# First stage of an encoder layer: lo parts and additions on VectorE alone, blocks of 2, 2, 4, 4, 4 k-tiles, modulation sums 512 columns wide

## The chip, the cores and the metric

The kernel runs on one core of a Trainium2 chip. The metric is the device time of one execution in microseconds (us). Three runs of the kernel before took 2361.72 to 2369.96 us, with a median of 2366.24 us. Engines are named as in the profile: PE is TensorE, DVE VectorE, ACT ScalarE, POOL GpSimd, SP SyncE (which issues the loads from HBM).

## The reference

One layer of an encoder for 512 tokens of width 2048, in float32. A condition vector c gives, through w_ada (2048 x 12288), six modulation vectors (shift, scale and gate for two sub-layers). The part at hand is the beginning:

```
mod = silu(c) @ w_ada + b_ada                       # 2048 -> 12288; sh1, sc1 are the first two parts
h = rms_norm(x, g_norm1) * (1 + sc1) + sh1          # 512 x 2048
proj = h @ w_in                                     # 2048 -> 3904: q, k, v of 8 heads, then the latents
```

Behind it stand differential attention (8 heads), latent attention (8 heads), the output projection, and a SwiGLU feed-forward network of width 5632 with its own norm and modulation.

## The kernel before

Every product of two float32 matrices is made from three products. Each factor is split into a part hi, rounded to the matmul's format (ScalarE casts it), and a rest lo = raw - hi, and the kernel sums hi x hi + lo x hi + hi x lo in PSUM (`mm3`, lines 240 to 243; for the activations the parts are called hh and hl). Weights come through the class `Weights`: `load` issues the DMA into one of three raw buffers, `split` casts hi and has lo subtracted on the engine that the plan names (line 98), `get` keeps one weight tile split ahead and one more loading. There are two buffers each for hi and lo. A weight tile of the first stage is [128, 2 k-tiles x 384 columns]: q, k and v of one head.

The modulation of the first norm is a matrix-vector product, made on VectorE. `ada_sum` (lines 292 to 311) loads w_ada in tiles of 128 x 1024 (512 KB, five buffers called araw) and adds each of the 16 row groups, scaled by an element of c, into an accumulator adaacc (line 308, the first of a sum by line 305). For a block of nk k-tiles the sum is nk x 128 columns wide, and there are two, scale and shift. TensorE then turns the sums into columns (`ada_columns`, line 327), VectorE makes G1 and SH1 from them (lines 328 to 330), and `modulation` transposes x for each k-tile (line 378), applies G1 and SH1 on ScalarE (line 380, xt), casts hh and subtracts hl (line 382).

The 16 k-tiles of the contraction go in blocks (`BLOCKS`), since the modulation of all of them would come too late. In each block the loop runs over five heads (`FIRST`); for each head `head_block` multiplies the block's k-tiles for four token tiles into four PSUM banks and adds the banks to what the head has so far (raw_in, raw_s). The first block is copied by ScalarE (line 486). In later blocks two of four token tiles are added by VectorE straight from PSUM (line 492) and two (`POOL_ADDS`) are copied by ScalarE (line 489) and added by GpSimd (line 490); in the last block all four are VectorE's. The last block is made only for head 0 here, and for heads 1 to 4 as filler within the attention of the heads before them.

Beside the matmuls of block i the loop spreads the sums of block i + 2 (generator `ahead`, over the first 0.9 of the block) and, from 0.2 of the block on, the columns, transposes and splits of block i + 1 (`near`). Before the loop come x, its norm, and the sums of the first two blocks.

Only TensorE's order is as written (`ORDERED`); the other engines' orders, and SyncE's queue of loads, are made by the framework's scheduler from the order of the code and expected times. Each engine then works through its own queue in order. TensorE's banks are in two sets of four that take turns from head to head (`next_tag`).

`W.busy` (line 669) is set to 8 when an attention head begins: the next eight weight tiles that the plan gives to GpSimd get their lo part from VectorE.

Of the kernel before, what the change touches and what calls it, by code (L numbers as in the profile page):

```python
# [10 lines left out]
F32 = mybir.dt.float32  # L11
F32R = mybir.dt.float32r
AF = mybir.ActivationFunctionType
ALU = mybir.AluOpType
# [4 lines left out]
P = 128  # L19
# [3 lines left out]
KC = D // P  # L23
# [13 lines left out]
T2_BUFS = 4  # L37
FIRST = 5
NEAR = 0.2
POOL_ADDS = (1, 3)  # L40
LOADS = "aaaxxxxaxxxxaxxxxaxxxxwaa"
BLOCKS = ((0, 2), (2, 2), (4, 2), (6, 2), (8, 2), (10, 2), (12, 4))
PARTS = (2, 4, 4, 4, 4, 4)
STRAIGHT = 2
X_SLOTS = 24
# [92 lines left out]
def weight_plan(a):  # L138
    w_in = a["w_in"][0]
    qkv = w_in[:, 0:3 * H * P].rearrange("(k p) (s n) -> p k s n", p=P, s=3)  # L140
    plan = []

    def rows(w, r0, nk, c0, n):
        return w[r0:r0 + nk * P, c0:c0 + n].rearrange("(k p) n -> p k n", p=P)

    def add_in(h, j):
        plan.append((("in", h, j), [2, 384], qkv[:, 2 * j:2 * j + 2, :, h * P:(h + 1) * P], "pool"))

    for k0, nk in BLOCKS:
        for h in range(FIRST):  # L150
            for j in range(k0 // 2, (k0 + nk) // 2):
                add_in(h, j)
    for h in range(FIRST, H):
        for j in range(KC // 2):
            add_in(h, j)
    c0 = 3 * H * P
    for i in range(2):
        for j in range(KC // 4):
            plan.append((("cq", i, j), [4, 256], rows(w_in, j * 512, 4, c0 + i * 256, 256), "pool"))
    for j in range(KC // 2):  # L160
        plan.append((("ckv", j), [2, 320], rows(w_in, j * 256, 2, c0 + QL, 320), "pool"))

    def add_out(b, j0, j1):
        for j in range(j0, j1):
            plan.append((("out", b, j), [2, 512], rows(a["w_out"][0], j * 256, 2, b * 512, 512), OUT_SPLIT))

    for pr in range(4):
        for j in range(2):
            plan.append((("qb", pr, j), [2, 384], rows(a["w_q_b"][0], j * 256, 2, pr * 384, 384), "pool"))
        plan.append((("kvb", pr), [2, 512], rows(a["w_kv_b"][0], 0, 2, pr * 512, 512), "pool"))  # L170
        if pr == 1:
            add_out(2, 0, 4)
        elif pr == 3:
            add_out(3, 0, 4)
    add_out(0, 0, 8)
    add_out(1, 0, 8)
    add_out(2, 4, 8)
    add_out(3, 4, 8)

    for j in range(STRAIGHT):  # L180
        for k4 in range(4):
            for n in ("gate", "up"):
                plan.append(((n, j, k4), [4, 256], rows(a["w_" + n][0], k4 * 512, 4, j * 256, 256), "alt"))
    return plan
# [14 lines left out]
def hybrid_layer(ctx, tc, a, out):  # L199
    nc = tc.nc  # L200
    act, dve, pool, pe, sp = nc.scalar, nc.vector, nc.gpsimd, nc.tensor, nc.sync
# [9 lines left out]
    def open_pool(name, side="left"):  # L211
        p = tc.tile_pool(name=name, bufs=1, reuse_waits="tile", side=side)
        return p, p.__enter__()
# [8 lines left out]
    def slot(name, dt=F32R):  # L222
        return big.tile([P, S], dt, tag="A", bufs=N_SLOTS, name=name)

    def bank(tag, name):
        return psum.tile([P, 512], F32, tag=tag, name=name)
# [3 lines left out]
    def next_tag():  # L230
        turn[0] ^= 1
        return "tmp" if turn[0] else "acc"

    def f(ap):
        return ap.bitcast(F32)

    def tsl(t):
        return slice(t * P, (t + 1) * P)
# [25 lines left out]
    st = open_pool("st")  # L264
# [56 lines left out]
    def ada_columns(sums, k0, nk, G, SH, cg, cbs, cbh):  # L321

        ks = slice(k0, k0 + nk)
        ps = bank(spare[0], "ps_ada")
        for i, acc in enumerate(sums):
            for m in range(nk):
                pe.matmul(ps[:, i * nk + m:i * nk + m + 1], acc[:, tsl(m)], ones, start=True, stop=True)
        dve.tensor_tensor(out=G[:, ks], in0=ps[:, 0:nk], in1=scol(cbs + k0, nk), op=ALU.add)
        dve.tensor_tensor(out=G[:, ks], in0=G[:, ks], in1=scol(cg + k0, nk), op=ALU.mult)
        dve.tensor_tensor(out=SH[:, ks], in0=ps[:, nk:2 * nk], in1=scol(cbh + k0, nk), op=ALU.add)  # L330
# [30 lines left out]
    last_hh = [None]  # L361
    sums1 = {k0: [] for k0, _ in BLOCKS}

    def modulation_sums(k0, nk):
        yield from ada_sums(raws0, accs0, 1, 0, k0, nk, 8 // nk, sums1[k0])

    def modulation(k0, nk):
        for b in range(1, 4):
            if k0 <= 4 * b - 2 < k0 + nk:
                with tc.issue_after(last_hh[0]):  # L370
                    for t in range(NT):
                        act.activation(xs[t][b], xs[t][b], AF.Copy, scale=rstd1[:, t:t + 1])
        ada_columns(sums1[k0], k0, nk, G1, SH1, C_G1, C_BSC1, C_BSH1)
        yield None
        for kc in range(k0, k0 + nk):
            ps = bank(spare[0], "ps_x")
            for t in range(NT):
                pe.transpose(ps[:, tsl(t)], xs[t][kc // 4][:, tsl(kc % 4)], ident)
            xt, hh, hl = slot("xt", F32), slot("hh"), slot("hl")
            act.activation(xt, ps, AF.Identity, scale=G1[:, kc:kc + 1], bias=SH1[:, kc:kc + 1])  # L380
            last_hh[0] = act.copy(out=hh, in_=xt).ins
            pool.tensor_tensor(out=hl, in0=xt, in1=f(hh), op=ALU.subtract)  # L382
            hT[kc] = (hh, hl)
            yield None

    first = modulation_sums(*BLOCKS[0])
    i = 0
    for kind in LOADS:
# [4 lines left out]
        else:  # L393
            t, b = divmod(i, 4)
# [35 lines left out]
    for t in range(NT):  # L430
        for b in range(4):
            sq = st[1].tile([P, 512], F32, tag="sq", bufs=2, name="sq1")
# [10 lines left out]
    def raw_tile(name="raw_in"):  # L443
        return sh[1].tile([P, 384], F32, tag="rin", bufs=16, name=name)
# [30 lines left out]
    raw_in = {}  # L475

    def head_block(h, k0, nk, tag, fine=False):

        pss = [bank(tag, "ps_in") for _ in range(NT)]
        yield from project(pss, hT, 384, [("in", h, j) for j in range(k0 // 2, (k0 + nk) // 2)], k0, nk,  # L480
                           fine=fine)
        if k0 == 0:
            raw_in[h] = [raw_tile() if h < 4 else slot("raw_s", F32)[:, :384] for _ in range(NT)]
        for t in range(NT):
            if k0 == 0:
                act.copy(out=raw_in[h][t], in_=pss[t][:, :384])
            elif t in POOL_ADDS and k0 + nk < KC:
                tm = st[1].tile([P, 512], F32, tag="sq", bufs=2, name="tm")[:, :384]
                act.copy(out=tm, in_=pss[t][:, :384])
                pool.tensor_tensor(out=raw_in[h][t], in0=raw_in[h][t], in1=tm, op=ALU.add)  # L490
            else:
                dve.tensor_tensor(out=raw_in[h][t], in0=raw_in[h][t], in1=pss[t][:, :384], op=ALU.add)  # L492

# [36 lines left out]

    for gen in (first, modulation(*BLOCKS[0]), modulation_sums(*BLOCKS[1])):
        for _ in gen:
            pass
# [6 lines left out]

    for i, (k0, nk) in enumerate(BLOCKS):
        final = i + 1 == len(BLOCKS)
        ahead = [modulation_sums(*BLOCKS[i + 2]) if i + 2 < len(BLOCKS) else iter(()), 0]
        near = [iter(()) if final else modulation(*BLOCKS[i + 1]), 0]
        heads = range(1 if final else FIRST)
        for h in heads:
            tag = next_tag()
            spare[0] = "tmp" if tag == "acc" else "acc"
            for j, _ in enumerate(head_block(h, k0, nk, tag)):
                at = (h + j / nk) / len(heads)  # L550
                run(ahead, 16, at, 0.0, 0.9)
                run(near, 7, at, NEAR, 0.95)
        for gen in (ahead[0], near[0]):
            for _ in gen:
                pass
        if i == 1:
            load_small()
            load_bias()
        if i == 2:
            use_small()  # L560
            lambda_scale()
            bias_strips()
# [486 lines left out]
    def tmp(name):  # L1049
        return fo[1].tile([P, S], F32, tag="tmp", bufs=4, name=name)  # L1050
# [25 lines left out]
    for b in range(4):  # L1076
        tag = next_tag()
        spare[0] = "tmp" if tag == "acc" else "acc"
        if b == 0:
            assert tag == "acc"  # L1080
            pss = half[0]
        else:
            pss = [bank(tag, "ps_o") for _ in range(NT)]
        j0 = 0 if b == 1 else 4
        for i, _ in enumerate(project(pss, mixT, 512, [("out", b, j) for j in range(j0, 8)], 2 * j0, KC - 2 * j0,
# [6 lines left out]
            if b == 1 and i % 2 and i < 16:  # L1092
                b2, t = 2 + i // 8, i % 8 // 2
# [8 lines left out]
        for t in range(NT):  # L1102
            residual(pss, b, t, gt1, pool if t in OUT_POOL and b < 3 else dve)
            sp.dma_start(out=x1d[t * P:(t + 1) * P, b * 512:(b + 1) * 512], in_=x1[t][b])
            sq = tmp("sq")
# [236 lines left out]
    for u in range(N_UNITS):  # L1342
# [4 lines left out]
        else:  # L1347
            ao = wp.tile([P, 1024], F32, tag="raw", bufs=3, name="ao").rearrange("p (c s) -> p c s", c=4)
            dve.tensor_tensor(out=ao, in0=g, in1=res, op=ALU.mult)
            j = u // 2 + STRAIGHT  # L1350
            sp.dma_start(out=actd[2 * j:2 * j + 2].rearrange("f p s -> p f s"),
                         in_=ao.rearrange("p (f c) s -> p f (c s)", f=2))
# [26 lines left out]
    j = 0  # L1379
    for i, n in enumerate(PARTS):  # L1380
        for b in range(4):
            tag = next_tag()
            spare[0] = "tmp" if tag == "acc" else "acc"
            pss = [bank(tag, "ps_d") for _ in range(NT)]
# [11 lines left out]
            for t in range(NT):  # L1396
# [8 lines left out]
                else:  # L1405
                    tm = fd[1].tile([P, S], F32, tag="x1r", bufs=4, name="tm")
# [65 lines left out]
```

## Time and profile before

| what | value |
| --- | --- |
| median of three runs | 2366.24 us |
| the profiled execution: its time, its span | 2365.25 us, 2363.4 us |
| TensorE matmul busy | 2215.7 us, 94% of the span |
| VectorE busy | 1680.8 us, 71% |
| ScalarE busy | 965.6 us, 41% |
| GpSimd busy | 591.3 us, 25% |
| moved by DMA | 345.02 MB, mean 146 GB/s |

The table counts the whole span. The first stage takes some 255 us of it, and its shares are other ones: what a change there is worth is read from that stretch alone. Busy times are unions of instructions; an instruction's own duration includes what it waits for inside the engine, so the start of one to the start of the next is the better measure of pace.

### The profile page before, as it was taken

How to read it: one execution, taken by the hardware profiler on the slowest of the kernel's cores; microseconds unless marked ns; L12 is line 12 of the kernel's file. 1: busy time of each engine (PE TensorE's matmuls, PEld its weight loads, DVE VectorE, ACT ScalarE, POOL GpSimd, SP SyncE). 2: the span in 40 equal slices, each digit the busy share in tenths (PEclk: the TensorE clock that was granted, in tenths of full speed). 3: DMA queues.
4: the chain of work that ended last, by engine and by line, in shares of the span. 5: the costliest groups of instructions: out<-in, count | busy, mean ns of one | idle time of the engine just before them, and what ended most of it. 6: DMA issues, size and time to landing. Idle time of an engine off the chain costs nothing.

```text
span 2363.4 us, 35665 instructions
## 1 busy us (share of the span) xinstructions
PE 2215.7 (94%) x13878; PEld 2012.5 (85%) x13878; DVE 1680.8 (71%) x2376; ACT 965.6 (41%) x1619; POOL 591.3 (25%) x591
## 2 busy tenths in 40 slices
PE   2878998999999997899999999999999998999999
PEld 2777998998778776779999999999999877888887
DVE  6999777877989567657777777777777677232543
ACT  4433555557555422444444444444444522121211
POOL 1668735335644241220000000000000122222221
PEclk9989999999999998999999999999999999999999
DMA  8765443632434278243333333333333686232442
GB/s 283 218 194 168 141 143 96 195 95 70 139 133 156 103 252 269 72 134 108 116 125 117 125 117 125 118 127 119 128 117 128 204 275 214 97 127 97 160 134 98
DMA packets 278764, 345.02 MB, mean 146 GB/s; under 512 B 14749, under 2 KB 187270, under 8 KB 278466
## 3 DMA queue, kind: packets, MB, share of 16 engines
q1 hardware_dynamic: 278104, 342.37, 44.6%
q8 instruction: 109, 1.79, 0.3%
q14 instruction: 61, 0.50, 0.1%
q10 hardware_dynamic: 490, 0.36, 0.1%
HBM read 322.71 MB, written 19.96 MB: 145 GB/s over the span
## 4 chain that ended last, share of the span: by engine, by line
PE 56%; DVE 5%; DMA 4%; issue 1%; ACT 0%; POOL 0%; SPq 0%; DVEq 0%; ACTq 0%; POOLq 0%
PE ps_d L243 6%; PE ps_d L242 6%; PE ps_d L241 6%; PE ps_X L1240 5%; PE ps_X L1239 5%; PE ps_X L1241 5%; PE ps_W L1239 3%; PE ps_W L1240 3%; PE ps_W L1241 3%; DVE adaacc L308 2%; DMA araw<-in_w_ada_dram 2%; PE ps_Z L1240 2%; PE ps_Y L1239 2%; PE ps_Y L1240 2%; PE ps_Z L1239 2%; PE ps_Z L1241 2%
## 5 line engine op out<-in xcount | busy, mean ns | idle before, releaser
L98 POOL TENSOR_TENSOR lo<-raw,hi 128x1024 fp32r<-128x1024 f32 (+1 forms) x108 | 249.2, 2308 | 1429.9 <-ACT hi L90 1406.4
L90 ACT CAST hi<-raw 128x1024 fp32r<-128x1024 f32 (+2 forms) x228 | 220.9, 969 | 455.0 <-PE ps_d L242 276.8
L241 PE MATMUL ps_in<-hi,hh 128*128 128x384 f32 (+2 forms) x704 | 242.7, 345 | 28.5 <-DVE raw_s L492 8.2
L1222 ACT CAST wh<-wr 128x1024 fp32r<-128x1024 f32 x160 | 168.5, 1053 | 244.3 <-PE ps_X L1240 68.3
L1240 PE MATMUL ps_X<-comb,wh 128*128 128x256 f32 x960 | 267.7, 279 | 0.0
L1241 PE MATMUL ps_X<-comb,wl 128*128 128x256 f32 x960 | 267.7, 279 | 0.0
L1239 PE MATMUL ps_X<-comb,wh 128*128 128x256 f32 x960 | 267.7, 279 | 0.0
L98 DVE TENSOR_TENSOR lo<-raw,hi 128x1024 fp32r<-128x1024 f32 (+2 forms) x120 | 138.3, 1152 | 174.8 <-ACT hi L90 174.0
L243 PE MATMUL ps_d<-lo,ax 128*128 128x512 f32 x640 | 253.6, 396 | 8.0 <-DVE lo L98 8.0
L308 DVE SCALAR_TENSOR_TENSOR adaacc<-araw,c_col,adaacc 128x256 f32<-128x256 f32 (+1 forms) x274 | 235.1, 866 | 33.3 <-DMA araw<-in_w_ada_dram 27.6
L242 PE MATMUL ps_d<-hi,ax 128*128 128x512 f32 x640 | 253.1, 396 | 0.0
L241 PE MATMUL ps_d<-hi,ax 128*128 128x512 f32 x640 | 253.1, 395 | 0.0
L1205 DVE TENSOR_TENSOR wl<-wr,wh 128x1024 fp32r<-128x1024 f32 x160 | 195.5, 1222 | 77.4 <-ACT wh L1222 77.3
L243 PE MATMUL ps_in<-lo,hh 128*128 128x384 f32 (+2 forms) x704 | 234.9, 334 | 8.7 <-POOL lo L98 8.7
L242 PE MATMUL ps_in<-hi,hl 128*128 128x384 f32 (+2 forms) x704 | 234.3, 333 | 1.0 <-POOL hl L382 0.9
L1222 ACT CAST wh<-wt 128x1024 fp32r<-128x1024 f32 x120 | 126.2, 1052 | 195.2 <-PE ps_X L1240 114.5
L1205 DVE TENSOR_TENSOR wl<-wt,wh 128x1024 fp32r<-128x1024 f32 x120 | 146.8, 1223 | 78.2 <-ACT wh L1222 78.1
L1240 PEld LDWEIGHTS ps_X<-comb,wh 128*128 128x128 f32 x960 | 180.5, 188 | 0.0
L1239 PEld LDWEIGHTS ps_X<-comb,wh 128*128 128x128 f32 x960 | 180.5, 188 | 0.0
L1241 PEld LDWEIGHTS ps_X<-comb,wl 128*128 128x128 f32 x960 | 180.5, 188 | 0.0
L1239 PE MATMUL ps_W<-comb,wh 128*128 128x256 f32 x640 | 179.1, 280 | 0.9 <-DVE cu L1250 0.8
L1240 PE MATMUL ps_W<-comb,wh 128*128 128x256 f32 x640 | 178.5, 279 | 0.0
(322 smaller groups left out, 5667.5 us busy)
## 6 DMA issues: line engine op xcount, KB each, us to landing
araw<-in_w_ada_dram SPq DMA_DIRECT2D x96, 512.0 KB
raw<-in_w_down_dram SPq DMA_DIRECT2D x88, 512.0 KB
wr<-in_w_gate_dram SPq DMA_DIRECT2D x40, 1024.0 KB
wr<-in_w_up_dram SPq DMA_DIRECT2D x40, 1024.0 KB
ada<-in_w_ada_dram SPq DMA_DIRECT2D x128, 256.0 KB
raw<-in_w_in_dram SPq DMA_DIRECT2D x128, 192.0 KB
raw<-in_w_out_dram SPq DMA_DIRECT2D x32, 512.0 KB
x<-in_w_ada_dram SPq DMA_DIRECT2D x64, 256.0 KB
```

Of the source, the lines that this page charges most:

```text
L90: nc.scalar.copy(out=hi[:, :n], in_=raw[:, :n])
L98: e.tensor_tensor(out=lo[:, :n], in0=raw[:, :n], in1=hi[:, :n].bitcast(F32), op=ALU.subtract)
L241: pe.matmul(o, ah, bh, start=start, stop=False)
L242: pe.matmul(o, al, bh, start=False, stop=False)
L243: pe.matmul(o, ah, bl, start=False, stop=stop)
L308: dve.scalar_tensor_tensor(out=acc[:, :width], in0=raw[:, i, :width], scalar=c_col[:, q:q + 1], in1=acc[:, :width], op0=ALU.mult, op1=ALU.add)
L1205: dve.tensor_tensor(out=out, in0=x, in1=y, op=ALU.subtract)
L1222: act.copy(out=hi, in_=src)
L1239: pe.matmul(ps[bk], wh[:, k], c[:, 0], start=first and k == 0, stop=False, skip_group_check=True)
L1240: pe.matmul(ps[bk], wh[:, k], c[:, 1], start=False, stop=False, skip_group_check=True)
L1241: pe.matmul(ps[bk], wl[:, k], c[:, 0], start=False, stop=k == 7, skip_group_check=True)
```

## The change

Three things change together.

1. `BLOCKS` becomes (0,2), (2,2), (4,4), (8,4), (12,4): five blocks instead of seven. The modulation sums of the third and fourth block are thereby 512 columns wide where they were 256; the first two stay at 256, the last is 512 wide in both. A tile of w_ada keeps its 512 KB and holds two row groups of 512 columns instead of four of 256.
2. The lo parts of the weights of the first five heads, and hl of all 16 k-tiles, are subtracted on VectorE instead of GpSimd. As these weight tiles no longer read "pool" in the plan, they no longer count down `W.busy`.
3. All additions of blocks go from PSUM on VectorE; the copies by ScalarE and the additions by GpSimd are gone.

```diff
-POOL_ADDS = (1, 3)
-BLOCKS = ((0, 2), (2, 2), (4, 2), (6, 2), (8, 2), (10, 2), (12, 4))
+BLOCKS = ((0, 2), (2, 2), (4, 4), (8, 4), (12, 4))
...
     def add_in(h, j):
-        plan.append((("in", h, j), [2, 384], qkv[:, 2 * j:2 * j + 2, :, h * P:(h + 1) * P], "pool"))
+        plan.append((("in", h, j), [2, 384], qkv[:, 2 * j:2 * j + 2, :, h * P:(h + 1) * P],
+                     "dve" if h < FIRST else "pool"))
...
-            pool.tensor_tensor(out=hl, in0=xt, in1=f(hh), op=ALU.subtract)
+            dve.tensor_tensor(out=hl, in0=xt, in1=f(hh), op=ALU.subtract)
...
-            elif t in POOL_ADDS and k0 + nk < KC:
-                tm = st[1].tile([P, 512], F32, tag="sq", bufs=2, name="tm")[:, :384]
-                act.copy(out=tm, in_=pss[t][:, :384])
-                pool.tensor_tensor(out=raw_in[h][t], in0=raw_in[h][t], in1=tm, op=ALU.add)
             else:
                 dve.tensor_tensor(out=raw_in[h][t], in0=raw_in[h][t], in1=pss[t][:, :384], op=ALU.add)
```

## Rows read from the trace of the kernel before

**Rows 1.** The page's 40 slices: busy tenths of TensorE and VectorE.
```profile
PE   2878998999999997899999999999999998999999
...
DVE  6999777877989567657777777777777677232543
```

**Rows 2.** Busy us by stretch: length; PE, PEld, DVE, ACT, POOL, clock, DMA share, GB/s.
```profile
38.70:226.70 188.00, 146.66 (x739) 135.03 (x738) 184.43 (x258) 73.66 (x128) 121.86 (x81) 0.91 0.68 207
226.70:244.20 17.50, 17.50 (x113) 17.18 (x112) 6.35 (x14) 10.83 (x19) 16.39 (x14) 1.00 0.26 70
244.20:255.00 10.80, 8.59 (x48) 7.95 (x47) 5.92 (x10) 4.77 (x12) 10.30 (x12) 1.00 0.76 225
255.00:300.00 45.00, 45.00 (x259) 44.33 (x259) 41.96 (x90) 22.14 (x52) 28.95 (x28) 0.96 0.41 121
```

**Rows 3.** VectorE's groups by form, 38.7 to 226.8 us: busy us, mean ns | idle before.
```profile
L308 DVE SCALAR_TENSOR_TENSOR adaacc<-araw,c_col,adaacc 128x256 f32<-128x256 f32 x149 | 117.6, 800 | 3.0
L308 DVE SCALAR_TENSOR_TENSOR adaacc<-araw,c_col,adaacc 128x512 f32<-128x512 f32 x30 | 40.5, 1352 | 0.5
...
L329 DVE TENSOR_TENSOR G<-G,small 128x2 f32<-128x2 f32 x6 | 1.6, 261 | 0.0
```

**Rows 4.** GpSimd's groups by form in the same stretch.
```profile
L98 POOL TENSOR_TENSOR lo<-raw,hi 128x768 fp32r<-128x768 f32 x27 | 53.5, 1983 | 29.0 <-ACT hi L90 24.6 <-PE ps_ada L327 4.3
L490 POOL TENSOR_TENSOR raw_in<-raw_in,tm 128x384 f32<-128x384 f32 x34 | 43.6, 1290 | 19.3 <-ACT tm L489 16.6 <-DMA araw<-in_w_ada_dram 2.6
L382 POOL TENSOR_TENSOR hl<-xt,hh 128x512 fp32r<-128x512 f32 x12 | 17.2, 1435 | 22.3 <-ACT hh L381 22.3
```

**Rows 5.** VectorE's groups by form, 75.5 to 87 us.
```profile
L308 DVE SCALAR_TENSOR_TENSOR adaacc<-araw,c_col,adaacc 128x256 f32<-128x256 f32 x10 | 11.8, 1183 | 0.4
```

**Rows 6.** VectorE's groups by form, 88 to 94 us.
```profile
L308 DVE SCALAR_TENSOR_TENSOR adaacc<-araw,c_col,adaacc 128x256 f32<-128x256 f32 x10 | 4.8, 483 | 0.3
```

**Rows 7.** Those two stretches: PE, PEld, DVE, ACT, POOL busy, clock, DMA share, GB/s.
```profile
75.50:87.00 11.50, 7.53 (x44) 7.21 (x42) 11.18 (x10) 3.67 (x7) 10.12 (x7) 1.00 0.54 167
88.00:94.00 6.00, 6.00 (x24) 5.90 (x24) 5.75 (x13) 0.36 (x1) 0.00 (x0) 0.50 0.88 254
```

**Rows 8.** VectorE's instructions in order of time: start, length, count.
```profile
7.33 5.69 DVE L308 SCALAR_TENSOR_TENSOR adaacc<-araw,c_col,adaacc 128x256 f32<-128x256 f32 x11
...
224.86 1.85 DVE L308 SCALAR_TENSOR_TENSOR adaacc<-araw,c_col,adaacc 128x512 f32<-128x512 f32 x1
226.63 1.93 DVE L492 TENSOR_TENSOR raw_in<-raw_in,ps_in 128x384 f32<-128x384 f32 x4
229.21 0.16 DVE L328 TENSOR_TENSOR G<-ps_ada,small 128x4 f32<-128x4 f32 x1 [0.65 <-PE ps_ada L327]
...
285.49 0.95 DVE L98 TENSOR_TENSOR lo<-raw,hi 128x768 fp32r<-128x768 f32 x1
286.36 0.75 DVE L697 SCALAR_TENSOR_TENSOR pm<-pm,cf 128x512 f32<-128x512 f32 x1
...
874.72 5.48 DVE L308 SCALAR_TENSOR_TENSOR adaacc<-x,c_col,adaacc 128x512 f32<-128x512 f32 x7
```

**Rows 9.** Instructions on the tile adaacc: ns min/median/max, first and last start.
```profile
L341 DVE TENSOR_TENSOR adaacc<-adaacc x4: 678/688/2471, 1912.1 to 1995.2; 128x512 fp32r<-128x512 f32 x4
```

**Rows 10.** TensorE's instructions in order of time.
```profile
63.30 0.33 PE L241 MATMUL ps_in<-hi,hh 128*128 128x384 f32 x1
63.48 0.33 PE L242 MATMUL ps_in<-hi,hl 128*128 128x384 f32 x1
```

**Rows 11.** Busy time by stretch, columns as in rows 2.
```profile
0.00:40.00 40.00, 3.90 (x17) 3.53 (x17) 20.15 (x47) 17.03 (x40) 3.37 (x7) 1.00 0.91 295
40.00:80.00 40.00, 33.33 (x170) 31.08 (x169) 38.54 (x59) 22.71 (x41) 18.69 (x12) 0.96 0.88 261
80.00:226.00 146.00, 111.33 (x561) 102.11 (x560) 143.96 (x196) 50.37 (x87) 102.46 (x69) 0.89 0.63 192
```

**Rows 12.** Waits of SyncE's queue, 0 to 300 us: total, times, longest.
```profile
SPq L301 <- DVE adaacc L308: 86.9, 45, 4.9
```

## The prediction

> **What bounds the kernel now.** I read the forty slices first, then the stretch of the first stage, then VectorE's groups in it. The slices (59 us each) [rows 1] show TensorE at nine tenths nearly everywhere but in the first four (2, 8, 7 and 8), and VectorE full in the second to fourth of them. So from about 240 us on TensorE sets the end and whatever the first stage gains is handed on; the first stage itself goes at VectorE's pace. By stretch [rows 2]: from 38.7 us (when the second block's sums begin) to 226.7 us (when the last modulation sum ends) VectorE is busy 184.43 of 188.00 us, TensorE 146.66. From 226.7 to 244.2, VectorE's sums being over, TensorE works without a gap and finishes the sixth block.
>
> What fills VectorE [rows 3]: 149 narrow sums (256 columns) at a mean of 800 ns and 30 wide ones (512) at 1352 ns. These means are not the instruction's own time. GpSimd works beside them for 121.86 us [rows 2], mainly on the lo parts, the additions and the hl parts [rows 4]. While GpSimd works, a narrow sum takes 1183 ns [rows 5]; while it does nothing, 483 ns [rows 6]; the two stretches differ in just that, 10.12 of 11.50 us of GpSimd against none [rows 7]. Additions read PSUM and stay at about 0.48 us in company too (four in 1.93 us, at 226.63 [rows 8]). So GpSimd takes from VectorE 149 x (0.800 - 0.517) + 30 x (1.352 - 0.783) = 42 + 17 = 59 us, with the chained pace of sums from [rows 8]: eleven narrow ones in 5.69 us, seven wide ones in 5.48 us.
>
> That this is a shared read port is the rule of the Trainium skill, SBUF — State Buffer, section "Who interferes with whom": an instruction with two SBUF inputs and a GpSimd instruction that reads SBUF exclude each other entirely. The trace agrees in kind, not in size: excluded entirely, the ten sums of [rows 5] (4.8 us by themselves) and 10.1 us of GpSimd would need 15 us and took 11.5. By the rule in full the change would free more than 59 us; the sum below goes by the measured pace alone.
>
> **The change part by part, to the last modulation sum.** Today it ends at 226.7 us (the sum at 224.86 in [rows 8]). Afterwards it belongs to the fifth block and is issued during the third (k-tiles 4 to 7). VectorE's queue from 38.7 us to there:
>
> 1. Sums left over from the second block, about 30 narrow: 30 x 0.517 = 15.5 us.
> 2. Sums of three blocks of four k-tiles, wide: 3 x 2 x 16 = 96 x 0.783 = 75.2 us. The columns are the same as in 192 narrow ones; those alone would be 99 us, so width is worth 24 us here. If they stand between other instructions the pace may be nearer to 0.67 us (64 us); beside a busy GpSimd it would be 1.35 (130 us).
> 3. Lo parts, new on VectorE: 5 heads x (1+1+2) = 20 in three blocks. One such took 0.95 us, 0.87 to the next start (285.49 and 286.36 in [rows 8]): 17.4 us. The other end is 20 x 1.98 [rows 4] = 40 us if they were as slow as on GpSimd; I take VectorE's own row.
> 4. hl parts, new: 12 for the k-tiles of blocks 2 to 4. The same form, 128x512 into fp32r, has a median of 688 ns [rows 9]: 8.3 us; as on GpSimd it would be 17.2.
> 5. Additions: in blocks two and three, 2 x 20 = 40 x 0.48 = 19.2 us, all on VectorE. By block count they fall (five old inner blocks had 100, the three new ones have 60).
> 6. Columns of G and SH, constants: some 5 us, as now (an estimate; the largest row is 1.6 us [rows 3]).
>
> Sum 140.6 us, so 179 us if the queue never idles. Today it idles 3.6 of 188 us.
>
> ScalarE loses the copies of the additions. It is busy 73.66 of 188 us, so this buys nothing. What the lo parts wait for (the cast to hi on ScalarE) stays.
>
> Next late is the DMA. Up to that point it must deliver x (4.2 MB), the two modulation parts (33.6 MB) and w_in for eight k-tiles of five heads (7.9 MB): 45.6 MB; 11.8 are there at 40 us (295 GB/s [rows 11]). The other 33.8 MB take 130 us at the 261 GB/s of 40 to 80 us, which ends at 170 us, hidden behind VectorE; at the 207 GB/s of the stretch today [rows 2] they take 163 us and end at 203. That present rate is VectorE's demand and no limit, so I take the former, with 4 us of idling as now and 3 us for the first wide block, where 10.4 MB (35 us at 295) meet about 32 us of VectorE work. So the last sum ends at 186 us: bounds 168 (with the pace of 0.67) and 203.
>
> **From the last sum to the end of the stage.** Behind it comes the fourth block (k-tiles 8 to 11, five heads). Matmuls of 384 columns start every 0.173 us [rows 10], so it is 5 x 4 x 12 x 0.173 = 41.5 us, and four groups of transposes at about 0.9 us. TensorE runs ahead of VectorE by at most a fifth of a block, because there the columns of G are due; it does so today (last sum 226.7, G at 229.21 [rows 8]). If it is ahead that far, 38 us remain; if it only just begins, 46. A lo part queued behind sums makes TensorE wait, and with all four additions on VectorE no bank comes free ahead of its queue, so I take the middle, 41. In that block VectorE has some 20 us of work in 41, so nothing there takes over. End: 186 + 41 = 227 us instead of 244.2, 17 us earlier. The last block of head 0 today takes 10.80 us with TensorE busy 8.59, with the lo parts still on GpSimd [rows 2]; 1.5 us more.
>
> Behind 255 us the edit adds little. The last lo parts of heads 1 to 4 go to VectorE already by W.busy; as they no longer use that count up, a few of head 5's follow, under 1 us each, beside a TensorE busy 45.00 of 45.00 us [rows 2]. VectorE there has 3 us free in 45, so the cost is between 0 and 5 us; fewer GpSimd reads repay some, and I take 0.
>
> The sum is -18.5 us: 2365.25 (the profiled execution, 1.85 us over its span) becomes 2346.7. That execution lies 1 us under the median of the runs, 2366.24, so I predict 2348 us; its own range is 2335 to 2358 for this case (last sum 177 to 191, and 38 to 46 behind it).
>
> **The rivals.**
>
> A. The loads become the bound. For it: VectorE's sums alone would take a 512 KB load every 1.57 us, 334 GB/s, more than any stretch in [rows 11]. Against: the additions, lo and hl parts stand between them. With the last sum at 203 us the block ends at 244, and the time is 2365. Chance 0.17.
>
> B. Slower: the queues lock together. Lo parts stand on VectorE behind sums that wait for loads; SyncE's queue waits today 86.9 us for VectorE to release modulation buffers [rows 12], and w_in's loads, whose three buffers will be released by the same VectorE, are in the same queue. A sum waiting for its load then holds the lo part that would release the next load. It decides at 207 GB/s: under it there is no gain. At the 192 GB/s that 80 to 226 us show [rows 11], 33.8 MB end at 216 us, the block at 257, and the time is 2377. For it: nothing outside VectorE will make a lo part any more. Against: by the code those buffers wait today for GpSimd's lo parts in the same manner. Chance 0.09.
>
> C. More gain: the wide sums at 0.67 us, the last at 168 us, TensorE a fifth ahead: 206, and 2326 us. TensorE's own work allows it (from 41 us on 8 x 5 x 12 x 0.173 = 83 us, a fifth of a block more, 8, and twelve groups of transposes, 11: 143 us). Chance 0.14.
>
> D. The long sums are not GpSimd's doing, and nothing is freed: 30 x 0.800 + 96 x 1.352 + 17.4 + 8.3 + 19.2 + 5 = 204 us, last sum at 242, 2403 us. Against it are [rows 5 to 7]. Chance 0.03. The Trainium skill, Perfetto Trace Analysis, section "Optimizing Scalar/DVE Operations", speaks on this side: a saturated VectorE should hand work to other engines, here the reverse is done; the same section warns that GpSimd may not help, as the two share a read port, and by the rows above the warning weighs more.
>
> **How the numbers follow.** The forecast has 0.57. What a measurement can tell from no change is 0.3%, 7 us. Faster: the forecast but for 0.02, and C, 0.69. Within: A and those 0.02, 0.19. Slower: B and D, 0.12. The range reaches from C to a little over A, 2326 to 2370.
>
> **What would show it.** Right: sums of 512 columns at 0.74 to 0.80 us; GpSimd nearly idle up to 230 us; VectorE's last sum of the stage between 175 and 195 us, head 4 of the fourth block done near 227; over 240 GB/s from 40 to 180 us; the same gaps as today behind 255 us. Wrong: sums still above 1 us (D); VectorE waiting for modulation loads by tens of us (A, B), with TensorE waiting for lo parts (B); or the stage ending early while TensorE shows new gaps behind it.

## The result and the profile after

The changed kernel takes 2328.54 us (median of four runs, 2325.06 to 2330.51) against 2364.84 us for the kernel before in the same runs: a ratio of 0.9838, 95% interval 0.9815 to 0.9861, so 36 us less. The forecast was 2348 us, 18 us less: the right way, inside the range, and half the size. Here and below, executions in the slower state are left out (one of the kernel before, one of the kernel with narrow sums). The profiled execution took 2330.51 us with a span of 2328.1 us.

The slices of the changed kernel's page, as [rows 1], with GpSimd's line:

```profile
PE   2799999999989997999999999999999999999999
...
DVE  6987777868898575847777777777777577232543
...
POOL 0002433445553622210000000000000221222221
```

GpSimd is out of the first three slices, and TensorE is at nine tenths or more from the third on, but for two slices. By stretch (columns as in [rows 2]): to the last modulation sum and the addition behind it, from there to the end of the fourth block, and the last block of head 0.

```profile
38.70:162.30 123.60, 104.84 (x575) 98.65 (x575) 119.89 (x211) 50.61 (x78) 0.00 (x0) 0.94 0.92 295
162.30:209.70 47.40, 47.36 (x283) 46.76 (x284) 27.77 (x52) 14.92 (x21) 4.75 (x7) 1.00 0.47 134
209.70:218.00 8.30, 8.30 (x50) 8.30 (x49) 8.16 (x15) 3.12 (x9) 0.00 (x0) 1.00 0.77 240
```

```profile
160.91 0.74 DVE L308 SCALAR_TENSOR_TENSOR adaacc<-araw,c_col,adaacc 128x512 f32<-128x512 f32 x1
161.57 0.54 DVE L488 TENSOR_TENSOR raw_s<-raw_s,ps_in 128x384 f32<-128x384 f32 x1
```

The last sum ends at 161.7 us (160.91 and 0.74), not at 226.7; the fourth block ends 48 us behind it, where the sixth block of the kernel before ended 17.5 us behind its last sum, since the fourth is twice as long; the last block takes 8.3 us instead of 10.8, without a gap. So the stage ends at 218.0 us where it ended at 255.0 [rows 2]: 37 us. VectorE's groups by form, from 38.7 to 162.3 us, against [rows 3]:

```profile
L308 DVE SCALAR_TENSOR_TENSOR adaacc<-araw,c_col,adaacc 128x512 f32<-128x512 f32 x90 | 66.4, 744 | 0.2
L97 DVE TENSOR_TENSOR lo<-raw,hi 128x768 fp32r<-128x768 f32 x20 | 19.0, 951 | 0.5 <-ACT hi L89 0.5
L488 DVE TENSOR_TENSOR raw_in<-raw_in,ps_in 128x384 f32<-128x384 f32 x32 | 17.4, 545 | 0.0
L308 DVE SCALAR_TENSOR_TENSOR adaacc<-araw,c_col,adaacc 128x256 f32<-128x256 f32 x28 | 12.7, 480 | 0.3
L382 DVE TENSOR_TENSOR hl<-xt,hh 128x512 fp32r<-128x512 f32 x12 | 8.2, 685 | 0.4 <-ACT hh L381 0.3
L488 DVE TENSOR_TENSOR raw_s<-raw_s,ps_in 128x384 f32<-128x384 f32 x8 | 4.3, 542 | 0.0
L305 DVE TENSOR_SCALAR adaacc<-araw,c_col 128x512 f32<-128x512 f32 x6 | 2.9, 478 | 0.0
```

The counts are those of the forecast (96 wide, 20 lo, 12 hl, 40 additions; 28 narrow for about 30). Not one form is slow any more: 744 ns for a wide sum that took 1352, 480 for a narrow one that took 800. What the durations hide is the pace. In order of time, at 100 us:

```profile
100.67 4.06 DVE L308 SCALAR_TENSOR_TENSOR adaacc<-araw,c_col,adaacc 128x512 f32<-128x512 f32 x6
104.65 0.68 DVE L382 TENSOR_TENSOR hl<-xt,hh 128x512 fp32r<-128x512 f32 x1
105.25 0.74 DVE L308 SCALAR_TENSOR_TENSOR adaacc<-araw,c_col,adaacc 128x512 f32<-128x512 f32 x1
105.91 0.54 DVE L488 TENSOR_TENSOR raw_in<-raw_in,ps_in 128x384 f32<-128x384 f32 x1
```

Six wide sums take 3.98 us up to the next instruction, 0.66 each, and so does the one at 105.25, which has an addition behind it: the next starts before the sum has ended. The six are not one chain: when a new sum began at 100.28 us, three instructions of the sum before it were still due (42 of 45), so the two sums most likely take turns. The seven of [rows 8] at 874.72 us, all on one accumulator, took 0.78.

Behind the stage the gain is handed on. The first scores of the attention (the tile ps_s; ns min/median/max, first and last start) start at 280.7 us before and at 241.1 after:

```profile
L683 PE MATMUL ps_s<-k,q x64: 388/393/774, 280.7 to 589.1; 128*128 128x512 f32 x64
```
```profile
L679 PE MATMUL ps_s<-k,q x64: 388/393/776, 241.1 to 549.4; 128*128 128x512 f32 x64
```

### The profile page after: what moved, and what is told of

It is laid out like the page before. It is cut to its first block, busy times and chain, and to the rows that moved or that the text cites. A ratio compares the mean times of both kernels' runs of the same rounds, so it can differ in the third digit from the quotient of the medians.

```text
span 2328.1 us, 35444 instructions
## 1 busy us (share of the span) xinstructions
PE 2208.3 (95%) x13878; PEld 2011.6 (86%) x13878; DVE 1634.0 (70%) x2365; ACT 944.7 (41%) x1569; POOL 442.9 (19%) x492
## 4 chain that ended last, share of the span: by engine, by line
PE 57%; DVE 6%; DMA 4%; issue 1%; ACT 1%; SPq 0%; POOL 0%; DVEq 0%; ACTq 0%
PE ps_d L243 6%; PE ps_d L241 6%; PE ps_d L242 6%; PE ps_X L1235 5%; PE ps_X L1236 5%; PE ps_X L1237 5%; PE ps_W L1235 3%; PE ps_W L1236 3%; PE ps_W L1237 3%; DVE adaacc L308 2%; DMA araw<-in_w_ada_dram 2%; PE ps_Y L1235 2%; PE ps_Z L1235 2%; PE ps_Y L1236 2%; PE ps_Z L1236 2%; PE ps_Z L1237 2%
## 5 line engine op out<-in xcount | busy, mean ns | idle before, releaser
L97 POOL TENSOR_TENSOR lo<-raw,hi 128x1024 fp32r<-128x1024 f32 (+1 forms) x75 | 183.6, 2448 | 1403.3 <-ACT hi L89 1384.5
L97 DVE TENSOR_TENSOR lo<-raw,hi 128x768 fp32r<-128x768 f32 (+2 forms) x153 | 168.5, 1101 | 188.5 <-ACT hi L89 184.2
L241 PE MATMUL ps_in<-hi,hh 128*128 128x384 f32 (+2 forms) x704 | 236.5, 336 | 6.1 <-ACT hi L89 2.7
L1237 PE MATMUL ps_W<-comb,wl 128*128 128x256 f32 x640 | 177.9, 278 | 0.0
```

The lines of the kernel that those rows point to most:

```text
L97: e.tensor_tensor(out=lo[:, :n], in0=raw[:, :n], in1=hi[:, :n].bitcast(F32), op=ALU.subtract)
L241: pe.matmul(o, ah, bh, start=start, stop=False)
L1237: pe.matmul(ps[bk], wl[:, k], c[:, 0], start=False, stop=k == 7, skip_group_check=True)
```

## The experiments

Each ratio is to the kernel before on the same chip; the changed kernel's is 0.9838. Where a stretch is compared, the first start on ps_s is taken (280.7 before, 241.1 after), since it lies right behind the stage; the end of the last sum is 226.7 before and 161.7 after.

**The engines alone.** The changed kernel with the seven old blocks.

```diff
-BLOCKS = ((0, 2), (2, 2), (4, 4), (8, 4), (12, 4))
+BLOCKS = ((0, 2), (2, 2), (4, 2), (6, 2), (8, 2), (10, 2), (12, 4))
```


> The kernel after with the seven old blocks, so only the engines change. Theory (GpSimd's reads hold VectorE up, and fewer, wider blocks then save VectorE more): VectorE's queue to the last sum is 158 narrow sums x 0.47 + 32 wide x 0.70 + 25 lo x 0.87 + 12 hl x 0.60 + 80 additions x 0.465 + 3 = 166 us, last sum near 209 us instead of 226.7, and 13 to 18 us gained in all: about 2350 us. Rival 1 (the gain is GpSimd's absence alone): the whole gain remains, 2329 us. Rival 2 (the gain is the blocks alone): 2365 us.

Measured: 2333.82 us, ratio 0.9862 (0.9834 to 0.9891). First scores at 246.8 us, last sum at 197.6. Most of the gain, so the first rival is nearer than my theory. The blocks add little, for with the old ones the last sum comes 36 us later than in the changed kernel, but the first scores follow 49 us behind it and not 79. VectorE's groups from 38.7 us to the last sum, and a piece in order of time:

```profile
L308 DVE SCALAR_TENSOR_TENSOR adaacc<-araw,c_col,adaacc 128x256 f32<-128x256 f32 x148 | 64.9, 478 | 0.4
...
L97 DVE TENSOR_TENSOR lo<-raw,hi 128x768 fp32r<-128x768 f32 x26 | 24.8, 954 | 1.9 <-ACT hi L89 1.9
L308 DVE SCALAR_TENSOR_TENSOR adaacc<-araw,c_col,adaacc 128x512 f32<-128x512 f32 x30 | 22.3, 749 | 0.0
```
```profile
120.16 0.48 DVE L308 SCALAR_TENSOR_TENSOR adaacc<-araw,c_col,adaacc 128x256 f32<-128x256 f32 x1
120.56 0.55 DVE L488 TENSOR_TENSOR raw_in<-raw_in,ps_in 128x384 f32<-128x384 f32 x1
```

A narrow sum with an addition behind it takes 0.40 us to the next start, not the 0.52 of the chain in [rows 8]. VectorE took on 43 additions (84 for 41), 26 lo and 12 hl parts, 43 x 0.465 + 26 x 0.87 + 12 x 0.60 = 50 us, and the last sum still came 29 us earlier: GpSimd's absence freed about 79 us, not 59. (The sums alone are 73 us shorter by their starts, 83.4 against 156.6 us.)

**The blocks alone.** The kernel before with the five new blocks.

```diff
-BLOCKS = ((0, 2), (2, 2), (4, 2), (6, 2), (8, 2), (10, 2), (12, 4))
+BLOCKS = ((0, 2), (2, 2), (4, 4), (8, 4), (12, 4))
```


> The kernel before with the five new blocks, engines as before: GpSimd still makes lo, hl and half the additions, so sums stay at about 0.8 us (narrow) and 1.3 us (wide) while it works. Theory: GpSimd has some 83 us of work up to the last sum instead of 122, VectorE loses 0.48 us to each of them, 40 us; with 92 us of its own the last sum ends near 175 us and about 20 us are gained: 2345 us. Rival 1 (engines alone): 2365 us. Rival 2 (blocks alone): 2329 us.

Measured: 2362.85 us, ratio 0.9987 (0.9975 to 0.9999): at most 0.3%. Of the three figures only the first rival's was met, yet the last sum came at 189.6 us, 37 earlier. Most of that goes into the block behind it, which is twice as long in these blocks: the first scores follow the last sum by 85 us here, by 79 in the changed kernel and by 54 before. So the stage gains 6 us (first scores at 274.4). The 20 us that I expected needed the last sum at 175: it came 14.5 us later. GpSimd worked 88 us up to there, and VectorE's sums took some 50 us more than at their pace in the changed kernel, where the expectation had 40. TensorE's waits and VectorE's (38 to 240 and to 227 us; total, times, longest):

```profile
PE ps_in L243 <- POOL lo L98: 15.7, 11, 4.3
PE ps_in L241 <- ACT hi L90: 9.9, 5, 2.8
PE ps_in L241 <- DVE small L425: 7.8, 1, 7.8
```
```profile
DVE raw_in L492 <- PE ps_in L243: 26.8, 10, 6.6
DVE G L328 <- PE ps_ada L327: 9.9, 4, 6.3
```

TensorE's wait for GpSimd's lo parts, 6.4 us in the same stretch of the kernel before, has grown to 15.7; VectorE waits for TensorE mostly behind its last sum (7 us of the 37 lie ahead of it).

**Narrow sums in the wide blocks.** Two accumulators of 256 columns in place of one of 512, for scale and shift; the loads then come in pieces of half the length.

```diff
-        yield from ada_sums(raws0, accs0, 1, 0, k0, nk, 8 // nk, sums1[k0])
+        for k in range(k0, k0 + nk, 2):
+            yield from ada_sums(raws0, accs0, 1, 0, k, 2, 4, sums1[k0])
...
```


> The kernel after, but the sums of the blocks of four k-tiles are made 256 columns wide, two accumulators for each of scale and shift: 192 narrow instructions instead of 96 wide ones, and pieces of 1 KB instead of 2 KB in the loads. Theory (up to some 113 us VectorE and the loads are both full, behind it TensorE): 192 x 0.47 against 96 x 0.70, 22 us more of VectorE before the last sum, 8 to 15 of them before 113 us: 2337 to 2343 us. Rival (the loads alone bind early, and width is worth nothing): within 3 us of the kernel after, 2329 us.

Measured: 2342.98 us, ratio 0.9911 (0.9883 to 0.9939): 14 to 17 us slower than the changed kernel, at or over the upper end of the forecast. The last sum ends at 179.4 us, 18 later; two narrow sums at 0.40 us stand for one wide one at 0.66, and VectorE's waits for the shorter pieces come to 1.1 us. In blocks of four k-tiles the width matters.

**GpSimd's reads back, for nothing.**

```diff
+        if self.spare is not None and self.plan[i][0][0] == "in" and self.plan[i][0][1] < FIRST:
+            h = hi[:, :n].bitcast(F32)
+            nc.gpsimd.tensor_tensor(out=self.spare[:, :n], in0=h, in1=h, op=ALU.subtract)
...
```


> The kernel after, and GpSimd makes a subtraction of 128 x 768 from each of the first five heads' hi parts into a tile that nobody reads: the reads and the length of the old lo parts, without anyone waiting for them. Theory: sums beside it take 0.8 to 1.4 us again; of 40 such subtractions some 11 lie before 113 us, 21 us of GpSimd at 0.48 us lost for each, 10 us; the later ones lie in VectorE's slack: 2336 to 2341 us. Rival (the long sums of before had another cause, and the gain is from work taken off the queue in front of TensorE): 2329 us and sums at 0.74 us.

Measured: 2356.82 us, ratio 0.9966 (0.9952 to 0.9981), 30 us slower than the changed kernel by the ratios: nearly four fifths of the gain gone, by work that no engine is seen to wait for up to the last sum. GpSimd's and VectorE's groups from 38.7 to 226 us:

```profile
L100 POOL TENSOR_TENSOR spare<-hi 128x768 f32<-128x768 f32 x28 | 50.3, 1797 | 140.7 <-ACT hi L89 140.7
```
```profile
L311 DVE SCALAR_TENSOR_TENSOR adaacc<-araw,c_col,adaacc 128x512 f32<-128x512 f32 x90 | 80.2, 898 | 0.2
L97 DVE TENSOR_TENSOR lo<-raw,hi 128x768 fp32r<-128x768 f32 x28 | 30.4, 1087 | 9.9 <-ACT hi L89 9.9
L492 DVE TENSOR_TENSOR raw_in<-raw_in,ps_in 128x384 f32<-128x384 f32 x46 | 25.0, 546 | 3.6 <-PE ps_in L246 3.5
```

Sums, lo and hl parts (hl 895 ns) get longer, additions from PSUM don't. The direction is the theory's. Its size is not: I expected the later reads to fall into slack and there was none. The last sum came at 187.8 us, 26 later, and all of that reached the end of the stage: first scores at 270.4 us, 29 later. Of the 28 subtractions 20 lie ahead of the last sum (38.7 to 187.8 us):

```profile
L100 POOL TENSOR_TENSOR spare<-hi 128x768 f32<-128x768 f32 x20 | 34.7, 1734 | 112.3 <-ACT hi L89 112.2
```

So 34.7 us of GpSimd cost 26, or 0.75 for each; longer instructions of VectorE make up 21 of the 26 us, idling the rest.

**The additions alone, and the lo and hl parts alone,** on the kernel before.

```diff
-POOL_ADDS = (1, 3)
+POOL_ADDS = ()
```


> The kernel before with all additions on VectorE; lo and hl parts stay on GpSimd, blocks stay. Theory now (what GpSimd takes from VectorE must be counted from the pace of sums in a mixed queue, 0.40 and 0.66 us, not from the chained pace, 0.52 and 0.78; that makes 0.66 us lost for each us of GpSimd): GpSimd loses 54 us up to the last sum, VectorE gets 36 us back and takes on 42 additions, 19.5 us: 16 us gained, about 2349 us. Rival (the chained pace, 0.48 lost for each): 6 us gained, 2358 us.


```diff
-... h * P:(h + 1) * P], "pool"))
+... h * P:(h + 1) * P], "dve" if h < FIRST else "pool"))
-            pool.tensor_tensor(out=hl, in0=xt, in1=f(hh), op=ALU.subtract)
+            dve.tensor_tensor(out=hl, in0=xt, in1=f(hh), op=ALU.subtract)
```


> The kernel before with lo and hl parts of the first stage on VectorE; half the additions stay with ScalarE and GpSimd, blocks stay. Theory (0.66): GpSimd loses 68 to 71 us, VectorE gets 46 back and takes on 29: 16 us gained, 2348 us; together with the additions alone this makes what the engines alone gave, 30 us. Rival 1 (0.48): 5 us, 2359 us. Rival 2 (GpSimd's lo parts were themselves the late link in front of TensorE): much more than half of the 30 us, 2340 us or less.

Measured: 2358.07 us, 0.9972 (0.996 to 0.9983), and 2346.36 us, 0.9924 (0.9906 to 0.9943); last sum at 217.7 and at 211.3 us. The parts came out as the theory had it, the additions as its rival had it; together 25 us of the 33 that the engines gave. So one figure of loss for each us of GpSimd is too simple.

**What binds early: VectorE or the loads?** One sum of the third block with each instruction twice; and, in another run, every second modulation load of the blocks of four left out (the tile before is used again).

```diff
+            times = 2 if raws is raws0 and part == p_scale and k0 == 4 else 1
...
+                    for _ in range(times):
...
```


> The kernel after, with each instruction of one sum (scale, third block, k-tiles 4 to 7) issued twice, 15 more wide ones, 10 to 12 us of VectorE in the stretch before 113 us; that sum comes out about doubled. If VectorE binds there: 9 to 12 us slower than the kernel after, 2338 to 2341 us. If the loads do (their share is 0.96 to 1.01 there) and VectorE only keeps step: 0 to 4 us, 2329 to 2333 us.


```diff
+            if not (half and j % 2):
                 raw = raws()
...
                 sp.dma_start(out=raw, in_=w_ada[:, nq * j:nq * (j + 1), col0:col0 + width])
...
```


> The kernel after, with every second load of the modulation sums left out in the blocks of four k-tiles (the tile before is used again), so VectorE has the same work and 12.6 MB less is loaded, up to 8 of them before 113 us. If the loads bind there: TensorE's waits between 75 and 113 us shrink, 5 to 15 us faster than the kernel after, 2314 to 2324 us. If VectorE's queue binds: within 3 us, 2326 to 2331 us.

Measured: 2340.83 us, 0.9900 (0.9877 to 0.9922), about 12 to 15 us slower; and 2327.46 us, 0.9846 (0.9826 to 0.9865), the same as the changed kernel. The stretch 80 to 113 us, of the changed kernel and of the one with half the loads:

```profile
80.00:113.00 33.00, 21.63 (x123) 20.43 (x122) 32.22 (x55) 12.05 (x17) 0.00 (x0) 0.86 0.95 310
```
```profile
80.00:113.00 33.00, 24.73 (x129) 24.02 (x128) 31.70 (x56) 11.00 (x16) 0.00 (x0) 0.84 0.57 173
```

The loads' share falls from 0.95 to 0.57 and VectorE stays full. The last sum does not come sooner for it (164.9 us against 161.7). A DMA share near one was no bound here: in the changed kernel SyncE's queue waits for VectorE to free the buffers of the modulation loads (0 to 260 us; compare [rows 12]), and from 38.7 us to its last sum no wait of VectorE's is one for a load.

```profile
SPq L301 <- DVE adaacc L308: 58.9, 44, 4.0
```

**And late?** The same doubling in the last sum.

```diff
+            times = 2 if raws is raws0 and part == p_scale and k0 == 12 else 1
```


> The kernel after, with each instruction of the last modulation sum of the scale (k-tiles 12 to 15) issued twice: 15 more wide instructions, 10 us of VectorE between 113 and 162 us; that sum comes out about doubled. TensorE works without a gap from 113 us on, and the columns of G come 15 us behind the last sum. If the last sum with what lies behind it sets the end (the form of the prediction), 10 us slower than the kernel after: 2339 us. If TensorE alone binds from 113 us on: 0 to 2 us, 2329 to 2331 us. If VectorE's queue still paces TensorE there through the lo parts that stand in it (it is busy 47.2 of 49.3 us): 4 to 10 us, 2333 to 2339 us.

Measured: 2339.03 us, 0.9896 (0.987 to 0.9923): 10 to 14 us slower. The last sum ends at 177.3 us, 16 later, and TensorE, which worked without a gap from 113 to 162.3 us in the changed kernel, waits 13.6 us for lo parts behind 113 us. So VectorE's queue binds up to its last sum; a full TensorE was in step with it, not ahead.

**Versions that go on from there.** Four blocks of four k-tiles, with the next block's columns from 0.7 or from 0.5 of a block on; in the first block a scaling of x is also moved behind the rest.

```diff
-NEAR = 0.2
+NEAR = 0.7
-BLOCKS = ((0, 2), (2, 2), (4, 4), (8, 4), (12, 4))
+BLOCKS = ((0, 4), (4, 4), (8, 4), (12, 4))
...
```


> The kernel after with four blocks of four k-tiles, all sums 512 columns wide; the columns of the next block are made from 0.7 of a block on instead of 0.2, since its sums are not there sooner. VectorE's queue loses 20 additions (9 us) and 64 narrow sums become 32 wide (5 us); the first block starts some 5 us later. Theory (VectorE's queue sets the first stage): 5 to 15 us faster than the kernel after, 2314 to 2324 us. Rival (the late start and the wait for the second block's sums cost as much): 2327 to 2335 us.

> As the kernel with four blocks, but the next block's columns from 0.5 of a block on. If the second block's sums are there by 0.7 of the first block's time only, TensorE waits for them at 0.5 some 5 to 8 us, once: 3 to 8 us slower than the one with 0.7. If they are there by then, the same within 2 us.

Measured: 2330.84 us, 0.9850 (0.9833 to 0.9868), and 2331.10 us, 0.9857 (0.9842 to 0.9872): nothing beyond the changed kernel, as the rival had it, and no difference between 0.7 and 0.5. TensorE's products start at 53.5 instead of 41.2 us, and then it stands still for one weight tile (in order of time, with the idle time before):

```profile
76.73 0.69 PE L241 MATMUL ps_in<-hi,hh 128*128 128x384 f32 x1 [17.69 <-ACT hi L89]
```

The third version is the one with 0.7, and issues the second block's sums inside the loop.

```diff
-    for gen in (first, modulation(*BLOCKS[0]), modulation_sums(*BLOCKS[1])):
+    for gen in (first, modulation(*BLOCKS[0])):
...
+        if i == 0:
+            todo.insert(0, BLOCKS[1])
+        ahead = [(s for k in todo for s in modulation_sums(*k)), 0]
...
```


> The kernel with four blocks (0.7), but the sums of the second block are issued within the loop over the first block instead of ahead of it. In the kernel with four blocks TensorE stands still once, 18.0 us at 58.7 us, until the second weight tile of head 0 is cast: its load is queued behind the second block's modulation loads. Theory: with the loads in the loop's order that wait goes, and as the last sum there ends at 160 us and TensorE works without a gap from 77 us on, 8 to 18 us are gained over the kernel with four blocks (2330.8 us): 2313 to 2323 us. Rival (the second block's sums come later by as much, and TensorE waits for its columns at 0.7 of the first block instead): 2326 to 2335 us.

Measured: 2322.34 us (2320.61 to 2324.80), 0.9825 (0.9811 to 0.9838), 6 us (by the ratios) to 8.5 us (by the medians) under the version with four blocks: the gap is gone (TensorE's longest wait for a cast is 1.8 us).

```profile
38.70:157.80 119.10, 101.72 (x572) 99.39 (x573) 108.97 (x166) 48.92 (x76) 0.00 (x0) 0.97 0.94 302
157.80:214.00 56.20, 56.20 (x330) 54.27 (x329) 32.64 (x65) 20.12 (x32) 3.20 (x7) 1.00 0.39 109
```

It is the fastest measured, 3 us (by the ratios) to 6 us (by the medians) under the changed kernel, but the intervals of the two ratios overlap: likely better, not shown beyond doubt.

## Why the prediction was wrong in size

**The bound was right.** VectorE's queue set the stage before, and sets it after: a sum made twice, some 10 us of instructions, costs 10 to 15 us whether early or late, and half the loads gain nothing. The form "last sum, and the block behind it" held in the changed kernel and in the one with its last sum doubled.

**The step that failed is the sum of VectorE's queue: 140.6 us, 147.6 with the waits put on top; up to the addition behind the last sum it took 123.6 with its waits.** The terms counted the right instructions at the wrong pace, the wide sums above all: 75.2 us were put for them and they took 63.3. Forecast and what the trace of after has, in us:

| term | forecast | after |
| --- | --- | --- |
| 30 (28) narrow sums | 15.5 | 11.9 |
| 96 wide sums | 75.2 | 63.3 |
| 20 lo parts | 17.4 | 17.4 |
| 12 hl parts | 8.3 | 7.2 |
| 40 additions | 19.2 | 18.6 |
| columns and constants | 5.0 | 1.5 |
| idling and waits, put on top | 7 | 3.7 |

The measured column takes starts from one instruction to the next, less the idle time between them: 0.66 us for a wide sum in the mixed queue (a few at 0.78), 0.40 to 0.52 for a narrow one, 0.87, 0.60 and 0.465 for the others. The last row is 123.60 less the 119.89 us busy, the one above it the rest. Half of what was off is the wide sums, 11.9 of 24 us. The forecast had both paces, took the chained one from [rows 8] and put 0.67 down as the bound. The right row was one in which the next instruction does not work on the same accumulator, which is what the change puts there. The sign "0.74 to 0.80 us" could not tell the two apart: a duration of 744 ns meets it, and the pace was 0.66.

**The same error sat in what GpSimd takes.** The forecast's 59 us came out as the mean less the chained pace. In a mixed queue the free pace is shorter, so the loss was larger: about 79 us by the run with the engines alone. With 50 us for what VectorE takes over, 29 us are left there in place of 9.

**Loads.** Forecast at 261 GB/s and hidden; they ran at 295 over the stretch and were hidden. The 4 us of idling came (3.7), the 3 us for the first wide block did not.

**From the last sum on.** Forecast 41 us between 38 and 46; it took 48. TensorE had no lead: the additions that end the third block stand among VectorE's last sums. That took 7 of the 24 us back which the earlier sum gave. The last block lost its waits for GpSimd, 2.5 us where 1.5 was forecast, and 0 was put for the attention, where 2 to 3 us more came (39.6 at the first scores, after 37.0 at the end of the stage).

**The rivals.** C had the last sum at 168, the block's end at 206 and 2326 us; measured were 162, 210 and 2328.5. Its pace of the sums was the case, and it got 0.14; that its time fits so well is in part luck, since the sums ended 6 us sooner still and TensorE was not a fifth of a block ahead. A and B fell with the half loads and with VectorE's waits, of which none from 38.7 us to the last sum is for a load. D fell with the run that puts GpSimd's reads back. That run was needed: the two stretches of [rows 7] do not differ in GpSimd alone, as the forecast has it, but also in ScalarE's work, the granted clock and the DMA share. The Trainium skill, Perfetto Trace Analysis, section "Optimizing Scalar/DVE Operations", cited with D, says of handing work over only that it may make sense; by the run with the engines alone, taking it back gained 33 us. On the rule of the Trainium skill, SBUF — State Buffer, section "Who interferes with whom": GpSimd's work does hold up the instructions with two SBUF inputs and leaves the additions from PSUM alone (546 ns with it, 545 without), as it states. Whether the two exclude each other entirely is not shown. The forecast's 15 us against 11.5 adds up GpSimd's durations, which are not fixed themselves (one and the same subtraction took 1.47 to 2.31 us in the run with its reads back); there 34.7 us of GpSimd moved the last sum by 26 us. No run tells GpSimd's reads from its writes.

**What stays open.** The feed-forward stretch took 6 us longer in the profile of after than in that of before, with no wait to show for it:

```profile
L1239 PE MATMUL ps_X<-comb,wh x960: 277/279/281, 1068.2 to 1848.3; 128*128 128x256 f32 x192
```
```profile
L1235 PE MATMUL ps_X<-comb,wh x960: 277/281/281, 1026.2 to 1812.0; 128*128 128x256 f32 x192
```

That is 780 against 786 us between first and last start. It does not follow the change: with the same code there, the profiled executions of all the kernels of this text lie between 778 us (half the loads) and 788 us (the blocks alone, whose engines are those of the kernel before), all at a granted clock of 1.00 and with at most 2.3 us of idle TensorE. Why TensorE's pace differs by 1% is open. Why the additions alone gave less for each us of GpSimd than the parts alone was not settled either.

## What to carry to other kernels

When an engine's instructions get shorter than their mean says, look up their pace, start to start, in a stretch whose neighbours are like those of the new queue; here a chain on one accumulator was the slow case (0.78 us for a wide sum, against 0.66). An engine off the path can cost the bound engine more than the work it takes over: here giving three kinds of work to a VectorE that was 98% busy made it finish 29 us sooner. And a full DMA or a TensorE without gaps next to a full VectorE proves nothing about who binds: halve one and double the other.

## What had not been expected

- Blocks alone moved the last sum 37 us earlier and the time by 0.1%: the block behind the last sum is longer by most of that.
- Wide sums at 0.66 us start to start with a duration of 0.74; narrow ones 0.40 with 0.48. In one chain 0.78 and 0.52.
- The DMA share was 0.95 at 310 GB/s without being the bound.
